# One-hot factors of a retrieval stage spread over three engines, and single dots tied to the cast stream

## The chip, the cores and the metric

The kernel runs on one core of a Trainium2 chip. The metric is the device time of one execution in microseconds (us). A core has TensorE (PE, matrix products; PEld is its loading of weights), VectorE (DVE), ScalarE (ACT), GpSimd (POOL) and SyncE (SP), each with its own queue of instructions that run in order, and DMA engines that are started from the queues of SP, ACT and POOL. Engines wait for each other by semaphores.

## The reference

A trunk of two layers over 256 tokens of width 1024. Each layer mixes tokens (gated convolution, window attention, spatial gating), then retrieves from 128 × 128 = 16384 single-neuron experts. Only the retrieval matters here:

```python
q = (t @ w_pq).reshape(T, PEER_HEADS, 2, PEER_HALF)
s = jnp.einsum('thpk,hpnk->thpn', q, sub_keys, preferred_element_type=jnp.float32)
top_s, top_i = lax.top_k(s, PEER_TOPK)
cand_s = top_s[:, :, 0, :, None] + top_s[:, :, 1, None, :]
cand_i = top_i[:, :, 0, :, None] * N_KEYS + top_i[:, :, 1, None, :]
best_s, best_pos = lax.top_k(cand_s.reshape(T, PEER_HEADS, PEER_TOPK * PEER_TOPK), PEER_TOPK)
experts = jnp.take_along_axis(cand_i.reshape(T, PEER_HEADS, PEER_TOPK * PEER_TOPK), best_pos, axis=-1)
gate = jax.nn.softmax(best_s, axis=-1)
u = expert_down[experts]
act = jax.nn.gelu(jnp.einsum('td,thkd->thk', t, u, preferred_element_type=jnp.float32), approximate=False)
wgt = (gate * act).astype(t.dtype)
vv = expert_up[experts]
return jnp.einsum('thk,thkd->td', wgt, vv)
```

For each token 8 heads choose 16 experts each: 128 pairs of a first index, a second index and a gate. The token's vector is multiplied with the chosen rows of one table, passed through a gelu, gated, and used to weight the chosen rows of another.

## The kernel before, in words

**The expert stage.** Instead of gathering rows, the kernel multiplies all tokens with all experts. The table "down" streams through in 128 chunks of 128 × 1024 (`next_chunk`, `chunk_mm`, L316 to L320). Each chunk is split into a high part (`hi`, a cast on ScalarE, L246) and a low part (`lo`, a subtraction on VectorE, L239), three buffers of each, and makes 24 matmuls: hi, lo and hi again (L318, L319, L320) for eight slices of the depth. `cast_step` makes the two parts, two chunks ahead of use, and gives them a high priority. SyncE fetches the raw chunks into seven buffers. Two chunks make a pair; after each pair ScalarE applies the gelu (`act`, `gelu`). The chunks of the conditioning weights that are due in the same stretch are held back and multiplied on VectorE right behind a low part (`Src.held`, `ada_chunk`, L204), where their place is pinned by `tc.keep_in_program_order`.

**The gates.** For 192 of the 256 tokens the chosen pairs are turned into a 128 × 128 matrix of gates per token, by a matmul of one-hots: the contraction runs over the token's 128 picks, one factor is the one-hot of the first index, the other the one-hot of the second index times the gate. The gate is kept as two 16-bit parts, high and low, so each token takes two matmuls (`gate_mm`, L1013 and L1014). Four tokens are a group; 48 groups a layer. `make_onehots` makes a group's one-hots into one of two buffers (`R_ON`): GpSimd compares the first index of each of the four tokens with a row of numbers (L1000, four instructions), VectorE compares the second index of all four in one instruction (L1003) and multiplies it with the high and with the low part (L1005, two instructions). `to_picks` (L866 to L871) transposes the picks of 128 tokens so that they lie across the partitions, in `picks` (32-bit) and `parts` (16-bit). `gate_use` multiplies the gate matrix into the activations, on VectorE (L1021) for experts that already have theirs and by a copy on ScalarE (L1024) for the rest. Groups are spread over the chunks from the one where the choosing is done (the list `fill` is empty) to chunk 124, at even chunks, some even chunks with two.

**The other 64 tokens** have their activations without gates written to memory (L1031) and are picked out per expert while the second table "up" streams through (`combine`). In layer 1 sixteen of them leave the big product (`FT` is 256 in layer 0 and 240 in layer 1); their chosen rows of "down" are gathered by GpSimd's indirect DMA (`dot_fetch`, L953, three buffers) and multiplied one by one on VectorE (`dot`, L959). `dot_plan` says at which chunk each step is issued: the fetches 5, 6 and 7 chunks after the gates' start, the first dot after 9, then one every 25/8 chunks, each followed by the fetch of the third next. `dot_where` (L948) makes the row numbers before.

**The order of the work.** In the expert stage's first half a planner fixes each engine's order: it simulates a timeline with its own costs and takes from what is ready the instruction of highest priority. So the place in the program is a priority and not a place in the queue, except for what is pinned. In the second half (`combine`) and at the seams the order is that of the program.

Of the kernel before, what the change touches and what calls it, by code (L numbers as in the profile page):

```python
# [17 lines left out]
P = 128  # L18
# [36 lines left out]
DOT_STEP = 25  # L55
# [3 lines left out]
def hybrid_trunk(ctx: ExitStack, tc: tile.TileContext, x_in, c_in, vec_in, w_ada, w_in, w_out, w_pq,  # L59
# [21 lines left out]
    iota = consts.tile([P, P], F16, name="iota")  # L81
    nc.gpsimd.iota(iota, pattern=[[1, P]], base=0, channel_multiplier=0,
                   allow_small_or_imprecise_dtypes=True)
# [13 lines left out]
    picks = consts.tile([P, S], F32, name="picks")  # L97
    parts = consts.tile([P, 3, S], F16, name="parts")
# [53 lines left out]
    R_DX = region(108 * S, D)  # L152
    R_DIX = region(127 * S + 128, 4, 16)
# [24 lines left out]
    class Src:  # L178
# [4 lines left out]
        held = []  # L183

# [34 lines left out]
    def cast_step(late=None):  # L219
# [13 lines left out]
        else:  # L233
# [20 lines left out]
            while Src.held:  # L254
                ada_chunk(*Src.held.pop(0), held=True)
        dma_ahead(k + RAW)
# [517 lines left out]
    def retrieval(layer, update, late):  # L774
# [80 lines left out]
        def to_picks(b):  # L855
# [10 lines left out]
            nc.vector.tensor_copy(picks[:, t], ps[:, 0:P])  # L866
            nc.scalar.copy(parts[:, 0, t], ps[:, P:2 * P])
            g = ps[:, 2 * P:3 * P]
            nc.scalar.activation(parts[:, 1, t], g, AF.Copy, scale=GATE_SCALE)
            nc.vector.scalar_tensor_tensor(parts[:, 2, t], g, GATE_SCALE, parts[:, 1, t],  # L870
# [53 lines left out]
    def experts(layer, rest):  # L924
# [32 lines left out]
        def dot(k):  # L957
            row = R_DOTS[k % 3]
            nc.vector.scalar_tensor_tensor(row, row, 1.0, R_DX, op0=OP.mult, op1=OP.mult,  # L959
                                           accum_out=R_DIX[:, 2, k:k + 1])  # L960
            if k + 3 < 16:
                dot_fetch(k + 3)
# [12 lines left out]
        def dot_plan(start):  # L975
            plan = {start: [lambda: nc.scalar.dma_start(dot_ids, chosen[P - alone:, 0, :])],
                    start + 2: [dot_ranks], start + 4: [dot_where]}
            for k in range(3):
                plan[start + 5 + k] = [lambda k=k: dot_fetch(k)]
            for k in range(16):  # L980
                plan.setdefault(start + 9 + k * DOT_STEP // 8, []).append(lambda k=k: dot(k))
            end = start + 9 + 15 * DOT_STEP // 8
            plan[end + 1] = [dot_acts]
            plan[end + 3] = [dot_back]
            assert end + 3 < 108
            return plan
# [5 lines left out]
        def make_onehots(g):  # L992
            tile4 = R_ON[g % 2]
            oh = tile4[:, 0].rearrange("p (i n) -> p i n", i=4)
            on = tile4[:, 1].rearrange("p (a n b) -> p a n b", a=2, b=2)
            og = [tile4[:, 2 + j].rearrange("p (a n b) -> p a n b", a=2, b=2) for j in range(2)]
            ts = slice(4 * g, 4 * g + 4)
            for i in range(4):
                t = 4 * g + i
                nc.gpsimd.tensor_scalar(oh[:, i, :], iota, picks[:, t:t + 1], None, op0=OP.is_equal)  # L1000
            wide = lambda j: parts[:, j, ts].rearrange("p (a b) -> p a b", b=2)[:, :, None, :].to_broadcast(
                [P, 2, P, 2])
            nc.vector.tensor_tensor(on, iota2[:, None, :, :].to_broadcast([P, 2, P, 2]), wide(0), op=OP.is_equal)  # L1003
            for j in range(2):
                nc.vector.tensor_tensor(og[j], on, wide(1 + j), op=OP.mult)  # L1005
            onehots[g] = oh, og

        def gate_mm(g):
            oh, og = onehots.pop(g)
            ps = bank("g", 2)  # L1010
            for i in range(4):
                dst = ps[:, i * P:(i + 1) * P]
                nc.tensor.matmul(dst, oh[:, i, :], og[0][:, i // 2, :, i % 2], start=True, stop=False)  # L1013
                nc.tensor.matmul(dst, oh[:, i, :], og[1][:, i // 2, :, i % 2], start=False, stop=True)  # L1014
# [343 lines left out]
```

## Time and profile before

| | us |
|---|---|
| median of three runs | 1742.49 (1738.18 to 1743.83) |
| the profiled execution | 1742.29 |
| its span in the profile | 1740.6 |
| PE busy | 1704.4 (98%) |
| DVE busy | 1454.9 (84%) |
| ACT busy | 905.4 (52%) |
| POOL busy | 868.1 (50%) |

The span runs from the first to the last instruction of the program. In it layer 0 chooses and multiplies with "down" from about 150 to 584 us and with "up" to about 880; layer 1 does so from about 1000 to 1432 and 1740. Gate matmuls run from 283 to about 569 and from 1129 to 1418. "A <- B" behind a group of instructions says that engine or line A sat idle until B ended. Matmuls are pipelined, so their durations overlap; where PE works without a pause the time from one to the next counts.

### The profile page before, as it was taken

To read this page: it belongs to the slowest core of one execution; us is meant where nothing else is said; L and a number is where in the kernel's file an instruction comes from. 1 tells how busy PE (TensorE), PEld (TensorE's weight loads), DVE (VectorE), ACT (ScalarE), POOL (GpSimd) and SP (SyncE) were. 2 spreads that over 40 slices of the span, in tenths; PEclk is the share of its full clock that TensorE was granted. 3 is DMA by queue.
4 is the path that set the end of the run, shared out by engine and by line. 5 is a ranking of instruction groups with operands and counts; after the bars stand their busy time and mean duration, and the time that the engine had idled before them with its cause. 6 is when DMAs were issued, how large, how long until landed. Compare 5 with 4: busy or idle time off the path is not lost.

```text
span 1740.6 us, 32411 instructions
## 1 busy us (share of the span) xinstructions
PE 1704.4 (98%) x11856; PEld 1555.4 (89%) x11856; DVE 1454.9 (84%) x2722; ACT 905.4 (52%) x1472; POOL 868.1 (50%) x713
## 2 busy tenths in 40 slices
PE   7999999999999999999999999998999999999998
PEld 6889999999999888888888999998999998888887
DVE  6858998788889699999966699968778878999996
ACT  2436455544444555555657555543554555555553
POOL 1000206588999377776100011259879847777630
PEclk9999999999999999999999999998999999999999
DMA  9965568888878799999954556687766668999993
GB/s 381 341 231 170 164 206 279 300 265 253 259 252 257 241 349 397 367 356 379 332 152 128 170 155 188 210 268 255 254 202 200 205 201 285 387 382 351 358 373 111
DMA packets 162562, 461.94 MB, mean 265 GB/s; under 512 B 51585, under 2 KB 53009, under 8 KB 161250
## 3 DMA queue, kind: packets, MB, share of 16 engines
q1 hardware_dynamic: 99936, 363.38, 61.6%
q0 software_dynamic: 26240, 88.36, 13.6%
q10 hardware_dynamic: 36226, 8.13, 2.2%
q8 instruction: 93, 1.52, 0.4%
q14 instruction: 67, 0.55, 0.1%
HBM read 449.16 MB, written 10.57 MB: 264 GB/s over the span
## 4 chain that ended last, share of the span: by engine, by line
PE 85%; DVE 9%; issue 2%; DMA 2%; POOL 1%; ACT 1%; SPq 0%; DVEq 0%; POOLq 0%; ACTq 0%
PE acc L1123 34%; PE ch L318 13%; PE ch L319 13%; PE ch L320 13%; PE ch L316 3%; DVE lo L239 3%; PE g L1013 1%; PE g L1014 1%; PE ch L399 1%; DMA raw<-in_w_ada 1%; PE acc L320 1%; PE acc L318 1%; PE acc L319 1%; DVE arena L781 1%; POOL arena L1000 1%
## 5 line engine op out<-in xcount | busy, mean ns | idle before, releaser
L246 ACT CAST hi<-raw 128x1024 fp32r<-128x1024 f32 x554 | 581.9, 1051 | 615.0 <-PE ch L320 314.4
L239 DVE TENSOR_TENSOR lo<-raw,hi 128x1024 fp32r<-128x1024 f32 x554 | 677.4, 1227 | 153.0 <-ACT hi L246 151.5
L318 PE MATMUL ch<-hh,hi 128*128 128x256 f32 (+1 forms) x2336 | 661.4, 283 | 0.1
L319 PE MATMUL ch<-hh,lo 128*128 128x256 f32 (+1 forms) x2336 | 656.2, 281 | 4.7 <-DVE lo L239 4.7
L320 PE MATMUL ch<-hh,hi 128*128 128x256 f32 (+1 forms) x2336 | 653.5, 280 | 0.0
L1000 POOL TENSOR_SCALAR arena<-iota,picks 128x128 f16<-128x128 f16 x384 | 445.9, 1178 | 184.4 <-PE g L1014 77.5
L319 PEld LDWEIGHTS ch<-hh,lo 128*128 128x128 f32 x2336 | 443.1, 190 | 6.5 <-DVE lo L239 6.1
L318 PEld LDWEIGHTS ch<-hh,hi 128*128 128x128 f32 x2336 | 442.9, 190 | 0.7 <-ACT ungated L1030 0.4
L320 PEld LDWEIGHTS ch<-hh,hi 128*128 128x128 f32 x2336 | 443.0, 190 | 0.0
L1123 PE MATMUL acc<-hi,hh 128*128 128x512 f32 x1536 | 400.6, 395 | 0.0
L1123 PEld LDWEIGHTS acc<-hi,hh 128*128 128x128 f32 x1536 | 288.6, 188 | 68.6 <-DVE hh L1064 0.2
L1123 PE MATMUL acc<-lo,hh 128*128 128x512 f32 x1024 | 281.2, 395 | 0.0
L1082 POOL DMA_INDIRECT arena<-in_up,arena x128 | 183.9, 1437 | 111.3 <-DVE arena L1119 84.6
L1123 PEld LDWEIGHTS acc<-lo,hh 128*128 128x128 f32 x1024 | 192.6, 188 | 45.8
L1089 POOL DMA_INDIRECT arena<-act_rows,arena x128 | 176.9, 1382 | 83.0 <-PE acc L1123 44.9
L1119 DVE SCALAR_TENSOR_TENSOR arena<-arena 128x1024 f32<-128x1024 f32 x126 | 161.9, 1285 | 0.0
L204 DVE SCALAR_TENSOR_TENSOR raw<-raw,arena 128x1024 f32<-128x1024 f32 x96 | 117.1, 1224 | 9.1 <-DMA raw<-in_w_ada 5.5
L1005 DVE TENSOR_TENSOR arena<-arena,parts 128x512 f16<-128x512 f16 x192 | 77.0, 440 | 23.0 <-PE g L1013 23.0
L795 POOL CAST arena<-arena 128x512 f16<-128x512 uint32 x32 | 27.1, 861 | 138.4 <-DVE arena L784 106.7
L759 POOL DMA_DIRECT2D arena<-in_keys x2 | 1.1, 562 | 170.7 <-issue 117.2
L1024 ACT ACTIVATE arena<-g 128x344 f32<-128x344 f32 (+23 forms) x96 | 31.1, 325 | 77.6 <-DVE arena L1021 76.0
L1013 PE MATMUL g<-arena 128*128 128x128 f16 x384 | 55.5, 223 | 7.8 <-POOL arena L1000 7.7
(243 smaller groups left out, 1666.5 us busy)
## 6 DMA issues: line engine op xcount, KB each, us to landing
raw<-in_down SPq DMA_DIRECT2D x256, 512.0 KB, 4.5
raw<-in_up SPq DMA_DIRECT2D x256, 512.0 KB, 6.4
raw<-in_w_ada SPq DMA_DIRECT2D x96, 512.0 KB, 4.7
raw<-in_w_pq SPq DMA_DIRECT2D x32, 512.0 KB, 3.9
raw<-in_w_in SPq DMA_DIRECT2D x26, 512.0 KB, 4.4
raw<-in_w_out SPq DMA_DIRECT2D x16, 512.0 KB, 3.9
act_rows<-ungated ACTq DMA_DIRECT2D x64, 64.0 KB, 4.7
arena<-in_w_in SPq DMA_DIRECT2D x6, 512.0 KB, 9.2
```

The costliest lines, as they stand in the source:

```text
L204: op = nc.vector.scalar_tensor_tensor(raw, raw, 1.0, cact, op0=OP.mult, op1=OP.mult, accum_out=mods[layer][:, col:col + 1])
L239: nc.vector.tensor_sub(lo, raw, hi.bitcast(F32))
L246: nc.scalar.copy(hi, raw)
L318: nc.tensor.matmul(dst, hi[:, cols], k[0], start=start, stop=False, **kw)
L319: nc.tensor.matmul(dst, lo[:, cols], k[0], start=False, stop=False, **kw)
L320: nc.tensor.matmul(dst, hi[:, cols], k[1], start=False, stop=stop, **kw)
L1000: nc.gpsimd.tensor_scalar(oh[:, i, :], iota, picks[:, t:t + 1], None, op0=OP.is_equal)
L1005: nc.vector.tensor_tensor(og[j], on, wide(1 + j), op=OP.mult)
L1082: nc.gpsimd.indirect_dma_start(out=R_ROWS[slots[k]], out_offset=None, in_=rows, in_offset=bass.IndirectOffsetOnAxis(ap=where_row[:, k:k + ...
L1089: nc.gpsimd.indirect_dma_start(out=R_ACTS[:, k % (2 * GROUP), :width - T], out_offset=None, in_=act_rows[layer][:, :], in_offset=bass.Indi ...
L1119: nc.vector.scalar_tensor_tensor(R_SUM, v, w8[:, k:k + 1], R_SUM, op0=OP.mult, op1=OP.add)
L1123: nc.tensor.matmul(acc[piece], w, u[:, lo:hi], start=piece not in opened, stop=last, skip_group_check=True)
```

## The change

- The order of the matmul's factors: the first index's one-hot now carries the gate parts (`og`), the second index's is plain (`on`).
- `picks` becomes 16-bit and holds both indices of a group side by side, so that one compare on VectorE makes both one-hots of the four tokens (1024 elements, `both`).
- The eight copies of the first index's one-hot with a gate part (four tokens, high and low) are made on three engines: GpSimd makes the high parts of tokens 0 and 1, each in one instruction that compares and multiplies (from `firsts` and `parts`, without waiting for the compare on VectorE); ScalarE makes the low parts of tokens 0 and 1 and the high parts of tokens 2 and 3 by a copy with a scale per partition; VectorE makes the low parts of tokens 2 and 3 in one multiplication. `parts` becomes 32-bit, as those operands are.
- `to_picks` writes these forms: two more small copies on ScalarE for each 128 tokens.
- The dots are issued by `cast_step`, behind the low part of the chunk being cast, and pinned there; one is handed over every 3 chunks from the 14th after the gates' start, and the first three fetches come 5, 8 and 11 chunks after it.

```diff
@@ consts
-    iota = consts.tile([P, P], F16, name="iota")
-    nc.gpsimd.iota(iota, pattern=[[1, P]], base=0, channel_multiplier=0,
-                   allow_small_or_imprecise_dtypes=True)
...
-    picks = consts.tile([P, S], F32, name="picks")
-    parts = consts.tile([P, 3, S], F16, name="parts")
+    picks = consts.tile([P, S // 4, 2, 4], F16, name="picks")
+    parts = consts.tile([P, 2, S], F32, name="parts")
...
+    firsts = region(127 * S, S // 4, 2)
@@ cast_step
             while Src.held:
                 ada_chunk(*Src.held.pop(0), held=True)
+            while Src.dots:
+                Src.dots.pop(0)()
@@ to_picks
-            nc.vector.tensor_copy(picks[:, t], ps[:, 0:P])
-            nc.scalar.copy(parts[:, 0, t], ps[:, P:2 * P])
+            at = picks[:, b * P // 4:(b + 1) * P // 4]
+            nc.vector.tensor_copy(at[:, :, 0, :], ps[:, 0:P].rearrange("p (g t) -> p g t", t=4))
+            nc.scalar.copy(firsts[:, b * P // 4:(b + 1) * P // 4, :],
+                           ps[:, 0:P].rearrange("p (g t) -> p g t", t=4)[:, :, 0:2])
+            nc.scalar.copy(at[:, :, 1, :], ps[:, P:2 * P].rearrange("p (g t) -> p g t", t=4))
             g = ps[:, 2 * P:3 * P]
-            nc.scalar.activation(parts[:, 1, t], g, AF.Copy, scale=GATE_SCALE)
-            nc.vector.scalar_tensor_tensor(parts[:, 2, t], g, GATE_SCALE, parts[:, 1, t],
+            high = tmp[:, 0, :].bitcast(F16)[:, :P]
+            nc.scalar.activation(high, g, AF.Copy, scale=GATE_SCALE)
+            nc.scalar.copy(parts[:, 0, t], high)
+            nc.vector.scalar_tensor_tensor(parts[:, 1, t], g, GATE_SCALE, high,
                                            op0=OP.mult, op1=OP.subtract)
@@ dot
-            nc.vector.scalar_tensor_tensor(row, row, 1.0, R_DX, op0=OP.mult, op1=OP.mult,
-                                           accum_out=R_DIX[:, 2, k:k + 1])
+            tc.keep_in_program_order(nc.vector.scalar_tensor_tensor(
+                row, row, 1.0, R_DX, op0=OP.mult, op1=OP.mult, accum_out=R_DIX[:, 2, k:k + 1]))
@@ dot_plan
             for k in range(3):
-                plan[start + 5 + k] = [lambda k=k: dot_fetch(k)]
+                plan[start + 5 + 3 * k] = [lambda k=k: dot_fetch(k)]
             for k in range(16):
-                plan.setdefault(start + 9 + k * DOT_STEP // 8, []).append(lambda k=k: dot(k))
-            end = start + 9 + 15 * DOT_STEP // 8
+                plan[start + 14 + 3 * k] = [lambda k=k: Src.dots.append(lambda: dot(k))]
+            end = start + 14 + 45
@@ make_onehots
             tile4 = R_ON[g % 2]
-            oh = tile4[:, 0].rearrange("p (i n) -> p i n", i=4)
+            both = tile4[:, 0:2].rearrange("p k (a n b) -> p (k a) n b", a=2, b=2)
+            vals = picks[:, g].rearrange("p k (a b) -> p (k a) b", b=2)
+            nc.vector.tensor_tensor(both, iota2[:, None, :, :].to_broadcast([P, 4, P, 2]),
+                                    vals[:, :, None, :].to_broadcast([P, 4, P, 2]), op=OP.is_equal)
+            oh = tile4[:, 0].rearrange("p (a n b) -> p a b n", a=2, b=2)
             on = tile4[:, 1].rearrange("p (a n b) -> p a n b", a=2, b=2)
-            og = [tile4[:, 2 + j].rearrange("p (a n b) -> p a n b", a=2, b=2) for j in range(2)]
-            ts = slice(4 * g, 4 * g + 4)
-            for i in range(4):
-                t = 4 * g + i
-                nc.gpsimd.tensor_scalar(oh[:, i, :], iota, picks[:, t:t + 1], None, op0=OP.is_equal)
-            wide = lambda j: parts[:, j, ts].rearrange("p (a b) -> p a b", b=2)[:, :, None, :].to_broadcast(
-                [P, 2, P, 2])
-            nc.vector.tensor_tensor(on, iota2[:, None, :, :].to_broadcast([P, 2, P, 2]), wide(0), op=OP.is_equal)
-            for j in range(2):
-                nc.vector.tensor_tensor(og[j], on, wide(1 + j), op=OP.mult)
-            onehots[g] = oh, og
+            og = [tile4[:, 2 + j].rearrange("p (a b n) -> p a b n", a=2, b=2) for j in range(2)]
+            t = 4 * g
+            for i in range(2):
+                nc.gpsimd.tensor_scalar(og[0][:, 0, i, :], iota2[:, :, 0], firsts[:, g, i:i + 1],
+                                        parts[:, 0, t + i:t + i + 1], op0=OP.is_equal, op1=OP.mult)
+                nc.scalar.activation(og[1][:, 0, i, :], oh[:, 0, i, :], AF.Copy,
+                                     scale=parts[:, 1, t + i:t + i + 1])
+                nc.scalar.activation(og[0][:, 1, i, :], oh[:, 1, i, :], AF.Copy,
+                                     scale=parts[:, 0, t + 2 + i:t + 3 + i])
+            nc.vector.tensor_tensor(og[1][:, 1], oh[:, 1],
+                                    parts[:, 1, t + 2:t + 4][:, :, None].to_broadcast([P, 2, P]), op=OP.mult)
+            onehots[g] = on, og
@@ gate_mm
-                nc.tensor.matmul(dst, oh[:, i, :], og[0][:, i // 2, :, i % 2], start=True, stop=False)
-                nc.tensor.matmul(dst, oh[:, i, :], og[1][:, i // 2, :, i % 2], start=False, stop=True)
+                for j in range(2):
+                    nc.tensor.matmul(dst, og[j][:, i // 2, i % 2, :], on[:, i // 2, :, i % 2], start=j == 0,
+                                     stop=j == 1)
```

More of the change, by code (lines that the diff above doesn't have):

```diff
@@ L54 @@
 FT = (S, 240)
-DOT_STEP = 25
 @with_exitstack
@@ L183, in hybrid_trunk @@
         held = []
+        dots = []
     def dma_ahead(upto):
@@ L993, in make_onehots @@
             tile4 = R_ON[g % 2]
-            oh = tile4[:, 0].rearrange("p (i n) -> p i n", i=4)
-            on = tile4[:, 1].rearrange("p (a n b) -> p a n b", a=2, b=2)
-            og = [tile4[:, 2 + j].rearrange("p (a n b) -> p a n b", a=2, b=2) for j in range(2)]
-            ts = slice(4 * g, 4 * g + 4)
-            for i in range(4):
-                t = 4 * g + i
-                nc.gpsimd.tensor_scalar(oh[:, i, :], iota, picks[:, t:t + 1], None, op0=OP.is_equal)
-            wide = lambda j: parts[:, j, ts].rearrange("p (a b) -> p a b", b=2)[:, :, None, :].to_broadcast(
-                [P, 2, P, 2])
-            nc.vector.tensor_tensor(on, iota2[:, None, :, :].to_broadcast([P, 2, P, 2]), wide(0), op=OP.is_equal)
-            for j in range(2):
-                nc.vector.tensor_tensor(og[j], on, wide(1 + j), op=OP.mult)
-            onehots[g] = oh, og
+            both = tile4[:, 0:2].rearrange("p k (a n b) -> p (k a) n b", a=2, b=2)
[3 more added lines that the diff above has]
+            oh = tile4[:, 0].rearrange("p (a n b) -> p a b n", a=2, b=2)
+            on = tile4[:, 1].rearrange("p (a n b) -> p a n b", a=2, b=2)
+            og = [tile4[:, 2 + j].rearrange("p (a b n) -> p a b n", a=2, b=2) for j in range(2)]
[10 more added lines that the diff above has]
+            onehots[g] = on, og
         def gate_mm(g):
-            oh, og = onehots.pop(g)
+            on, og = onehots.pop(g)
             ps = bank("g", 2)
```

## The prediction

> **What bounds the kernel now.** I read the busy shares first, then the waits, then the time in stretches of whole chunks. A chunk is the 24 matmuls of one block of 128 expert rows (eight depth slices, three products each); in the expert stage it is the unit of time.
>
> ```profile
> span 1740.6 us, 32411 instructions
> ## 1 busy us (share of the span) xinstructions
> PE 1704.4 (98%) x11856; PEld 1555.4 (89%) x11856; DVE 1454.9 (84%) x2722; ACT 905.4 (52%) x1472; POOL 868.1 (50%) x713
> ```
>
> PE is the bound; an edit on other engines can only win back what PE stands idle or runs slowly. So I looked for where it does. In the next view the columns after the stretch are its length and each engine's busy time with its count, then the granted clock and the DMA share.
>
> ```profile
> core 0: us, PE busy (x) PEld busy (x) DVE busy (x) ACT busy (x) POOL busy (x), PEclk, DMA share, GB/s
> 271.00:569.00 298.00, 298.00 (x2667) 296.19 (x2667) 256.64 (x442) 147.79 (x287) 239.58 (x196) 1.00 0.83 268
> 1093.91:1118.03 24.12, 24.12 (x218) 24.12 (x217) 24.05 (x59) 12.10 (x19) 0.00 (x0) 1.00 0.71 213
> 1121.00:1148.88 27.88, 27.76 (x251) 27.50 (x250) 19.91 (x37) 16.86 (x27) 17.26 (x13) 1.00 0.61 183
> 1148.88:1178.38 29.50, 26.62 (x236) 25.65 (x235) 22.32 (x35) 13.47 (x26) 18.04 (x12) 1.00 0.92 328
> 1178.38:1233.35 54.97, 47.19 (x413) 45.27 (x410) 43.80 (x80) 21.82 (x44) 52.65 (x46) 0.91 0.79 255
> 1239.24:1275.06 35.82, 35.82 (x348) 35.64 (x346) 26.86 (x48) 18.73 (x38) 27.70 (x29) 1.00 0.69 210
> 432.40:470.51 38.11, 38.11 (x346) 37.86 (x345) 33.93 (x60) 18.49 (x37) 33.09 (x27) 1.00 0.83 260
> ```
>
> The first row is the whole gate stage of layer 0: PE has no idle time at all, and the last row, twelve chunks of it, none either. The row 1239 to 1275 is the settled gate stage of layer 1, the same. Between them lies the loss: from 1148.88 to 1233.35, where layer 1's dots and its first gate groups run. The waits name two causes.
>
> ```profile
> engine line waited for: us in total, times, longest us
> ACT hi L246 <- PE ch L320: 314.4, 244, 6.1
> ...
> POOL arena L1000 <- PE g L1014: 77.5, 33, 17.1
> ACT arena L1024 <- DVE arena L1021: 76.0, 82, 2.9
> ...
> DVE arena L959 <- DMA arena<-in_down_rows,arena: 13.1, 8, 3.8
> ...
> POOL arena L953 <- DVE arena L959: 9.8, 6, 3.0
> PEld L1013 <- POOL arena L1000: 9.4, 8, 2.1
> ...
> PEld ch L319 <- DVE lo L239: 6.1, 7, 1.9
> ```
>
> Gate matmuls (L1013) wait for GpSimd's compares (L1000), eight times; and chunks wait for low parts (L239), while a dot (L959) stands ahead of them on VectorE waiting for its gathered rows. The chain of waits shows the same stretch from the other side:
>
> ```profile
> 1155.74 8.26 DMA arena<-in_down_rows,arena
> ...
> 1188.51 1.42 POOL arena L1000
> 1201.34 2.86 POOL arena L1000 x2
> ...
> 1205.48 1.83 POOL arena L1000
> ```
>
> **How large the loss is.** A chunk without gates takes 24.12/9 = 2.68 us (second row: nine chunks). In the settled stretch of layer 1, twelve chunks and seven gate groups take 35.82, so a group adds (35.82 − 12 × 2.68)/7 = 0.52. The stretch from 1148.88 holds nine chunks and two groups: 24.12 + 1.04 = 25.2 expected, 29.50 taken, **4.3 lost**. The one from 1178.38 holds fourteen chunks and nine groups: 37.5 + 4.7 = 42.2 expected, 54.97 taken, **12.8 lost**. Of these 12.8, 54.97 − 47.19 = 7.8 is PE standing idle; the other 5.0 is the clock, granted at 0.91 here and at 1.00 in every other row (0.09 × 54.97 = 4.9). All told 17.1 can be won, and 0.6 more from 1121.00 (ten chunks and one group, 27.3 expected, 27.88 taken), which I leave alone. By the Trainium skill ("TensorE: Matmul & The Clock Gate", Part 1) the clock drops to half after an idle window of about 3.4 us and returns after a busy one of that length; with it the 5.0 would go as soon as the idle stretches go, which is how I count it from the rows anyhow, and short leftover waits would cost only themselves.
>
> **Why GpSimd is late there, and what the change does to it.**
>
> ```profile
> L1000 POOL TENSOR_SCALAR arena<-iota,picks x384: 590/872/2768, 272.6 to 1413.6; 128x128 f16<-128x128 f16 x192
> ...
> L953 POOL DMA_INDIRECT arena<-in_down_rows,arena x16: 937/1674/1872, 1148.4 to 1212.1; - x16
> ...
> DMA to landing us min/median/max: 4.4/6.9/8.8
> ```
>
> ```profile
> L1000 POOL TENSOR_SCALAR arena<-iota,picks 128x128 f16<-128x128 f16 x384 | 445.9, 1178 | 184.4 <-PE g L1014 77.5 <-DVE picks L866 53.9 <-DVE arena L849 52.5
> ...
> L1005 DVE TENSOR_TENSOR arena<-arena,parts 128x512 f16<-128x512 f16 x192 | 77.0, 440 | 23.0 <-PE g L1013 23.0
> ...
> L1003 DVE TENSOR_TENSOR arena<-iota,parts 128x512 f16<-128x512 f16 x96 | 42.1, 449 | 0.0
> ...
> L843 DVE TENSOR_TENSOR arena<-arena 128x1024 f16<-128x1024 f16 x8 | 5.4, 678 | 0.0
> ...
> L415 DVE TENSOR_TENSOR arena<-arena 128x256 f32<-128x256 f32 x18 | 6.5, 419 | 0.0
> ...
> L563 ACT ACTIVATE arena<-arena,m 128x128 f32<-128x128 f32 x16 | 6.2, 391 | 5.2 <-DVE m L560 5.2
> ...
> L1030 ACT ACTIVATE ungated<-ch 128x128 f32<-128x128 f32 x64 | 17.6, 276 | 0.0
> ```
>
> GpSimd's compare takes 0.59 at best, 1.18 in the mean. A group needs four: 4.71 us. A group comes every 35.82/7 = 5.1 us, so GpSimd is at its limit even without dots, and each dot puts a row fetch of 1.67 on the same queue, which moreover waits for the dot three before it (9.8 in all). That is the 12.8.
>
> *GpSimd after:* two instructions a group, each a compare and a multiplication. No row shows a two-operation form. Below: the mean of one operation, 1.18; above: twice that, 2.36. The 0.59 beyond the best case is time that some other instruction held it up, and that doesn't double with the work in it, so the inside is 0.59 to 1.18 plus 0.59; I take 1.5. A group is then 3.0 instead of 4.71 (bounds 2.4 to 4.7), and with a fetch of 1.67 every three chunks (0.96 a group) still under 5.1. By the Trainium skill ("GPSIMD Engine Reference", section 3.1) up to two operations per element are limited by the port and cost what one does; no run here shows it; by it a group would be 2.4 and nothing of the 12.8 would stay.
>
> *VectorE after:* one compare of 1024 elements (0.68, L843) and one multiplication of 256 with a 32-bit factor (0.42, L415; not below 0.22, half of L1005) replace 0.45 + 2 × 0.44 = 1.33. That is 1.10, or 22 us less busy time over 96 groups, all behind a busy PE: nothing won.
>
> *ScalarE after:* four activations with a per-partition scale a group: 0.39 each (L563 has such an operand; L1030 without one is the lower end at 0.28), so 1.1 to 1.56. In the settled stretch of layer 1 that makes 18.73 + 7 × 1.56 = 29.7 of 35.82 (83%), in layer 0 18.49 + 10.9 = 29.4 of 38.11 (77%). It is hidden behind PE as long as casts come in time. The cover is the third buffer of `hi`: the slot is free when the chunk three before has ended (the 314.4 us of waiting above), and its low part is needed two chunks later.
>
> ```profile
> L239 DVE TENSOR_TENSOR lo<-raw,hi 128x1024 fp32r<-128x1024 f32 x554 | 677.4, 1227 | 153.0 <-ACT hi L246 151.5
> L246 ACT CAST hi<-raw 128x1024 fp32r<-128x1024 f32 x554 | 581.9, 1051 | 615.0 <-PE ch L320 314.4 <-PE acc L1123 147.9 <-DVE lo L239 99.5
> ...
> L959 DVE SCALAR_TENSOR_TENSOR arena<-arena x16: 1211/1224/1451, 1154.2 to 1217.7; 128x1024 f32<-128x1024 f32 x16
> L959 DVE DVE_READ_ACCUMULATOR arena<-arena x16: 76/78/84, 1155.4 to 1218.8; 128x1 f32 x16
> ```
>
> Two chunks are 5.36 at least; cast and low part take 1.05 + 1.23; 3.1 is to spare in layer 1.
>
> *New waits.* ScalarE's four now wait for VectorE's compare, which waits for PE to have left the buffer; behind them on ScalarE stand the next cast, the gelu and the gating copy (L1024, already waiting 76.0 in all). PE's gate matmuls wait for three engines instead of two. I charge 0.5 us in all for this, with 0 and about 5 (96 groups by 0.05) as ends.
>
> *Dots.* They leave the time when the planner had packed sixteen of them into 65 us (1154 to 1219) and come one per three chunks, each behind a low part that was due anyway. A dot's rows have three buffers, so some nine chunks or 25 us to arrive, against 6.9 to land: the 13.1 of waiting should go, and with it the 4.3. The single wait for the row numbers ahead of the first fetch stays; I leave 0.5 for it. The dots now fall on the settled gate stage: VectorE there becomes 26.86 − 1.6 + 4 × 1.30 (L959 with the reading of its sum) = 30.5 of 35.82, still hidden. I charge 1.0 for collisions.
>
> *The rest:* two more small copies at each of the four evacuations of the picks, on ScalarE at half load (16.86 of 27.88): nothing. The gate matmuls are as many and of the same shapes: nothing. Layer 0: nothing to win, the first row says.
>
> **The sum.** The profiled execution took 1742.3 (span 1740.6 and 1.7 around it); the median shown is 1742.5, so it stands for the runs. 1742.3 − 12.8 − 4.3 + 0.5 + 0.5 + 1.0 = 1727.2; I keep 1.3 of the 12.8 as not recovered, since the end of the dots (their write and read back on ScalarE's queue) lay inside it and only moves: **1728.5**. Its own range is 1722 to 1736.
>
> **Rivals.**
>
> *GpSimd stays last.* If the joint operation costs the upper end, 2.36, a group still takes 4.7, and with a fetch of 0.96 a group that is 5.7 against 5.1: the gate matmuls wait as before while the dots last. For it: no row shows such an instruction, and GpSimd's times range from 590 to 2768 ns. Against: the part beyond 0.59 is delay, not work. Only the 4.3 is won: 1742.3 − 4.3 = 1738.0, no change that can be told. 14%.
>
> *ScalarE's queue becomes the delay (slower).* Place: a group of layer 1 whose compare stands on VectorE behind a low part and a dot. Then ScalarE's four start after 1.23 + 1.30 + 0.68 and hold the next cast until 1.56 later: 4.8, which is 1.7 over the 3.1 to spare, and PE stands for it at L319. Sixteen dots make 27: 1728.5 + 27 = 1755.5; from twelve such groups on it is slower than before by what can be told. For: ScalarE at 83%, in order, and waits chained over three engines. Against: the planner places the four where it expects the compare done, and casts go ahead by priority. 13%.
>
> *The dots do not do what is said.* Only the dot is pinned, not its fetch; if fetches slip behind GpSimd's one-hots, VectorE waits at a fixed place, as the 13.1 did. It costs the 4.3 again: 1732.8, inside the forecast's range.
>
> **How the numbers follow.** Forecast with its range 73%, GpSimd last 14%, ScalarE late 13%. A difference under 0.3% (5.2 us, 1737.3 to 1747.7) can't be told here. Of the second case a little falls under 1737.3. So faster 0.74, same 0.13, slower 0.13. The range goes from 1721 (everything regained, with a few microseconds of scatter) to 1744, which takes in the second case and the small ends of the third.
>
> **What would show it.** Right: in layer 1 the stretch of the first ten or so gate groups has PE busy throughout at a clock of 1.00; no row of L1013's successor waits for GpSimd by more than 1 us in all; the dots lie about 8 us apart; GpSimd's instruction is near 1.5 in the mean; layer 0's gate stage still takes 298 for the same chunks. Wrong: GpSimd's mean over 2.2, or casts that wait for VectorE's compare with PE idle at the low-part matmul, or gaps at the gate matmuls ended by ScalarE.

## The result and the profile after

The changed kernel takes 1724.25 us (median; 1723.44 to 1725.37) against 1743.16 us for the kernel before on the same chip: a ratio of 0.9896, with a 95% interval from 0.9875 to 0.9918. The forecast was 1728.5 us with a range from 1721 to 1744. The profiled execution took 1724.26 us.

First the profile of after, its span and busy shares:

```profile
span 1722.6 us, 32340 instructions
...
PE 1696.9 (99%) x11856; PEld 1552.3 (90%) x11856; DVE 1440.4 (84%) x2626; ACT 1015.3 (59%) x1864; POOL 714.0 (41%) x520
```

PE issues the same 11856 matmuls. ScalarE is 110 us busier and GpSimd 154 us less busy, but neither was the bound. What counts is where PE stops losing time. Here are the stretches of after that answer to those shown of before, in the same columns (length, each engine's busy time, granted clock, DMA share): layer 0's gate stage, nine or ten chunks without gates, then three stretches of layer 1 in which gate groups run.

```profile
core 0: us, PE busy (x) PEld busy (x) DVE busy (x) ACT busy (x) POOL busy (x), PEclk, DMA share, GB/s
271.00:569.00 298.00, 298.00 (x2665) 295.89 (x2664) 253.37 (x407) 202.51 (x483) 150.79 (x100) 1.00 0.83 268
1093.00:1118.00 25.00, 25.00 (x226) 25.00 (x225) 20.75 (x49) 12.10 (x19) 0.00 (x0) 1.00 0.72 221
1148.00:1174.00 26.00, 26.00 (x244) 25.91 (x243) 14.86 (x24) 16.31 (x36) 7.31 (x7) 1.00 0.77 262
1176.92:1216.32 39.40, 39.40 (x386) 39.20 (x385) 29.54 (x49) 29.37 (x70) 18.91 (x16) 1.00 0.69 221
1222.22:1257.86 35.64, 35.64 (x345) 35.46 (x343) 30.33 (x50) 26.48 (x66) 29.71 (x19) 1.00 0.78 257
```

In layer 1 PE now works without a gap at a clock of 1.00 where it stood idle for 10.7 us of 84.5 before. In layer 0 the same 298 us hold practically the same number of matmuls (2665 and 2667).

The waits of after that concern the change:

```profile
POOL arena L1008 <- PE g L1024: 194.7, 62, 21.7
...
ACT arena L1010 <- DVE arena L1001: 32.8, 73, 1.9
...
DVE arena L1001 <- PE g L1024: 19.0, 29, 1.4
...
POOL arena L958 <- DVE arena L964: 4.5, 2, 2.3
```

GpSimd waits for PE now (L1008 is its compare with factor, L1024 the gate matmul), not PE for GpSimd: no wait of PE names L1008 at all. VectorE's dots (L964) have no wait for their rows either.

How long the two expert stages take from end to end is read from the high-part matmul's weight loads: the last two numbers before the form are the start of the first and of the last one. First before, then after:

```profile
L318 PEld LDWEIGHTS ch<-hh,hi x2336: 186/188/333, 149.6 to 1431.4; 128*128 128x128 f32 x195
```
```profile
L318 PEld LDWEIGHTS ch<-hh,hi x2336: 186/188/194, 149.7 to 1414.6; 128*128 128x128 f32 x195
```

That is 1281.8 before and 1264.9 after: 16.9 us of the 18.0 between the two profiled executions. The rest lies behind the last chunk, where 309.2 us (1740.6 − 1431.4) became 308.0. In the profiles of the ten experiments below this tail takes between 308.0 and 309.5 us, with the change and without it, so I do not put the 1.2 us down to the change. I call the time between the two starts "the expert stages" from here on.

### The profile page after: what moved, and what is told of

It is laid out like the page before. It is cut to its first block, busy times and chain, and to the rows that moved or that the text cites. A ratio compares the mean times of both kernels' runs of the same rounds, so it can differ in the third digit from the quotient of the medians.

```text
span 1722.6 us, 32340 instructions
## 1 busy us (share of the span) xinstructions
PE 1696.9 (99%) x11856; PEld 1552.3 (90%) x11856; DVE 1440.4 (84%) x2626; ACT 1015.3 (59%) x1864; POOL 714.0 (41%) x520
## 4 chain that ended last, share of the span: by engine, by line
PE 88%; DVE 9%; DMA 1%; ACT 1%; issue 1%; SPq 0%; DVEq 0%; ACTq 0%
PE acc L1134 35%; PE ch L318 14%; PE ch L319 13%; PE ch L320 13%; PE g L1024 3%; PE ch L316 3%; DVE lo L237 3%; PE ch L399 1%; DMA raw<-in_w_ada 1%; PE acc L318 1%; PE acc L320 1%; PE acc L319 1%; DVE arena L781 1%; DVE arena L782 1%; DVE arena L784 1%; PE acc L316 1%
## 5 line engine op out<-in xcount | busy, mean ns | idle before, releaser
L318 PE MATMUL ch<-hh,hi 128*128 128x256 f32 (+1 forms) x2336 | 660.7, 283 | 0.0
L318 PEld LDWEIGHTS ch<-hh,hi 128*128 128x128 f32 x2336 | 441.2, 189 | 0.3 <-issue 0.3
L1008 POOL TENSOR_SCALAR arena<-iota,arena,parts 128x128 f16<-128x128 f16 x192 | 293.1, 1534 | 307.9 <-PE g L1024 194.7
L1093 POOL DMA_INDIRECT arena<-in_up,arena x128 | 180.1, 1407 | 111.5 <-DVE arena L1130 81.7
L1100 POOL DMA_INDIRECT arena<-act_rows,arena x128 | 180.5, 1410 | 85.3 <-issue 35.6
L1010 ACT ACTIVATE arena<-arena,parts 128x128 f16<-128x128 f16 x192 | 75.6, 395 | 33.7 <-DVE arena L1001 32.8
L1001 DVE TENSOR_TENSOR arena<-iota,picks 128x1024 f16<-128x1024 f16 x96 | 68.0, 710 | 19.1 <-PE g L1024 19.0
L1012 ACT ACTIVATE arena<-arena,parts 128x128 f16<-128x128 f16 x192 | 74.2, 388 | 0.0
```

The lines of the kernel that those rows point to most:

```text
L318: nc.tensor.matmul(dst, hi[:, cols], k[0], start=start, stop=False, **kw)
L1008: nc.gpsimd.tensor_scalar(og[0][:, 0, i, :], iota2[:, :, 0], firsts[:, g, i:i + 1], parts[:, 0, t + i:t + i + 1], op0=OP.is_equal, op1=OP. ...
L1010: nc.scalar.activation(og[1][:, 0, i, :], oh[:, 0, i, :], AF.Copy, scale=parts[:, 1, t + i:t + i + 1])
L1093: nc.gpsimd.indirect_dma_start(out=R_ROWS[slots[k]], out_offset=None, in_=rows, in_offset=bass.IndirectOffsetOnAxis(ap=where_row[:, k:k + ...
L1100: nc.gpsimd.indirect_dma_start(out=R_ACTS[:, k % (2 * GROUP), :width - T], out_offset=None, in_=act_rows[layer][:, :], in_offset=bass.Indi ...
```

## The experiments

All kernels do the whole computation unless the expectation says otherwise. Times are medians; the ratio is to the kernel before on the same chip. The expert stages are read from the row shown above in each kernel's own profile.

| run | time, us | ratio to before (95%) | expert stages, us |
|---|---|---|---|
| before | 1740.7 to 1743.2 | 1 | 1281.8 |
| after | 1724.25 | 0.9896 (0.9875 to 0.9918) | 1264.9 |
| 1 dots alone | 1737.16 | 0.9977 (0.9965 to 0.9988) | 1280.1 |
| 2 one-hots alone | 1744.02 | 1.0006 (0.9993 to 1.0019) | 1285.0 |
| 3 before without dots | 1735.02 | 0.9963 (0.9949 to 0.9978) | 1265.1 |
| 4 after, dots not pinned | 1741.23 | 0.9997 (0.9980 to 1.0014) | 1279.8 |
| 5 after, dots pinned, old places | 1724.36 | 0.9899 (0.9883 to 0.9916) | 1266.3 |
| 6 GpSimd's copies twice | 1795.54 | 1.0308 (1.0282 to 1.0335) | 1336.9 |
| 7 all eight copies on ScalarE | 1728.34 | 0.9923 (0.9901 to 0.9944) | 1269.2 |
| 8 dots in both layers | 1715.47 | 0.9843 (0.9825 to 0.9862) | 1257.9 |
| 9 as 8, GpSimd none | 1712.82 | 0.9839 (0.9819 to 0.9858) | 1253.6 |
| 10 as 8, GpSimd one copy | 1710.87 | 0.9824 (0.9806 to 0.9843) | 1251.2 |

**1. The dots alone** (the kernel before, with the dots' new places and their pin):

```diff
+            while Src.dots:
+                Src.dots.pop(0)()
...
-            nc.vector.scalar_tensor_tensor(row, row, 1.0, R_DX, ...)
+            tc.keep_in_program_order(nc.vector.scalar_tensor_tensor(row, row, 1.0, R_DX, ...))
-                plan[start + 5 + k] = [lambda k=k: dot_fetch(k)]
+                plan[start + 5 + 3 * k] = [lambda k=k: dot_fetch(k)]
-                plan.setdefault(start + 9 + k * DOT_STEP // 8, []).append(lambda k=k: dot(k))
+                plan[start + 14 + 3 * k] = [lambda k=k: Src.dots.append(lambda: dot(k))]
```

> The kernel before with the dots alone moved: behind low parts, pinned, one per three chunks; the one-hots as before (four compares on GpSimd). Theory A, two causes (the prediction's): GpSimd needs 4 x 1.18 = 4.71 us a group, and with a row fetch of about 1.4 every three chunks (0.8 a group) 5.5 against the 5.1 that a group may take, so gate matmuls go on waiting for GpSimd, now spread over the 130 us that the dots take: 0.4 x 26 groups = 10 lost, 4.3 won and 3 to 6 more: about 1735 to 1739. Theory B, one cause, the crowding of the dots: GpSimd with four compares is good enough wherever dots do not crowd it (layer 0 has no idle time with it), so nearly all of the 17 is won by moving the dots: 1726 to 1728, PE busy throughout in the first gate groups of layer 1, clock 1.00 there.

Measured: 1737.16 us, as theory A has it. The first gate groups run clean, and the loss comes back later, where two gate groups fall together among the dots: all twelve waits of gate matmuls for GpSimd lie at the four such places between 1252 and 1368 us. In the windows of this kernel, the first gate groups and then two such places with their neighbours:

```profile
1176.00:1216.00 40.00, 40.00 (x384) 39.82 (x383) 31.37 (x57) 21.18 (x42) 32.06 (x32) 1.00 0.66 214
...
1246.00:1262.00 16.00, 13.96 (x118) 13.21 (x117) 10.65 (x21) 6.45 (x13) 15.64 (x17) 0.89 0.68 224
1318.00:1334.00 16.00, 13.96 (x119) 13.19 (x118) 11.00 (x20) 6.22 (x13) 15.60 (x17) 0.89 0.67 221
```

and its waits (L1003 is GpSimd's compare here, L1016 the gate matmul):

```profile
PEld L1016 <- POOL arena L1003: 9.9, 13, 1.5
...
PE g L1016 <- POOL arena L1003: 7.5, 12, 1.3
```

GpSimd is busy for 15.6 of 16 us there and PE waits for it, 7.5 us in all; behind three of the four places the trace shows the clock at half for 3.4 us, which costs another 5.1. So beside the pinned dots four compares a group are still too much. The prediction's sum for GpSimd (5.7 us a group against 5.1) had the shortage in every group; it shows only where two groups come together.

**2. The one-hots alone** (the changed kernel with the dots as before: neither pinned nor moved; the reverse of the diff above):

> The changed kernel with the dots as before (unpinned, fetches at 5, 6 and 7, a dot per 25/8 chunks from the ninth, placed by the planner), the one-hots on three engines. Theory A: the 12.8 is GpSimd's load and goes, the 4.3 of dots that wait for their rows ahead of low parts stays: 1743 - 12.8 = 1730, gaps only ahead of low-part matmuls. Theory B: the crowding stays, VectorE is as full as before while sixteen dots stand in 65 us, and the gate matmuls now wait for VectorE's compare and ScalarE instead of GpSimd: 1736 to 1742.

Measured: 1744.02 us: nothing gained, and more than either theory had. Its waits (L963 is the dot, L238 the low part, L318 its matmul):

```profile
DVE arena L963 <- DMA arena<-in_down_rows,arena: 17.9, 8, 6.6
...
PEld ch L318 <- DVE lo L238: 15.7, 7, 4.1
...
PE ch L318 <- DVE lo L238: 14.4, 7, 4.0
```

PE no longer waits for GpSimd; it waits 14.4 us for low parts instead, against 4.7 in before. One case from the timelines of VectorE and PE in this kernel (start, length, idle time before and its releaser in brackets):

```profile
1165.20 1.23 DVE L963 SCALAR_TENSOR_TENSOR arena<-arena 128x1024 f32<-128x1024 f32 x1 [6.56 <-DMA arena<-in_down_rows,arena]
...
1166.55 1.21 DVE L238 TENSOR_TENSOR lo<-raw,hi 128x1024 fp32r<-128x1024 f32 x1
```
```profile
1167.82 0.38 PE L318 MATMUL ch<-hh,lo 128*128 128x240 f32 x1 [3.18 <-DVE lo L238]
```

The dot stands on VectorE for 6.56 us until its rows have come; the low part that PE needs stands behind it, in order; PE waits 3.18 us. This kind of gap was known from before (13.1 us of such waits), but the faster one-hots did not leave it at 4.3 us: all of the loss is in it now. Every kernel is planned anew, though (the first dot starts at 1165.2 us here, at 1154.2 in before). How much of the 14.4 lay hidden behind GpSimd's waits in before, and how much the new order made, these runs do not separate.

**3. Before without the dots** (no row fetches, a small fill in place of each multiplication):

```diff
-            nc.vector.scalar_tensor_tensor(row, row, 1.0, R_DX, ..., accum_out=R_DIX[:, 2, k:k + 1])
-            if k + 3 < 16:
-                dot_fetch(k + 3)
+            nc.vector.memset(R_DIX[:, 2, k:k + 1], 0.0)
...
-                plan[start + 5 + k] = [lambda k=k: dot_fetch(k)]
+                pass
```

> The kernel before without the sixteen row fetches and their multiplications in layer 1 (sums set to zero; the sixteen tokens' part of the output is left out). Both theories: the dots are needed for the loss, so the stretch from layer 1's first gate group on runs without idle time though GpSimd still makes four compares a group: 1743 - 17 = 1726 (1724 to 1728). A third, that GpSimd's compares or the seam of the choosing alone cause waits there, expects a part of the 12.8 to stay: 1730 or more, with gate matmuls that wait for GpSimd.

Measured: 1735.02 us, but the time alone misleads: this kernel reaches its first expert chunk 9.8 us later than before (159.4 against 149.6), because the planner put the first transfers in another order (its chain of waits begins with `vec` and `w_in`, that of before with `w_ada`). The expert stages take 1265.1 us, as after. So four compares a group, with no dots, lose nothing:

```profile
L318 PEld LDWEIGHTS ch<-hh,hi x2336: 186/188/193, 159.4 to 1424.5; 128*128 128x128 f32 x195
```
```profile
1131.00:1183.00 52.00, 51.87 (x471) 51.59 (x470) 34.14 (x55) 30.29 (x52) 26.62 (x20) 1.00 0.72 241
1183.00:1226.00 43.00, 43.00 (x417) 42.77 (x417) 31.87 (x59) 22.49 (x44) 31.11 (x33) 1.00 0.66 205
```

Four compares without dots cost nothing, then; unpinned dots cost the whole even beside the lighter one-hots (run 2); pinned dots beside four compares still cost most of it (run 1). The loss needs the dots, and with them it goes only when both are seen to.

**4 and 5. Pin or place?** Run 4 keeps the new places in the plan, but the dots are neither handed to the cast nor pinned; run 5 keeps the pin, behind the low part, at the old places.

```diff
 run 4
-            tc.keep_in_program_order(nc.vector.scalar_tensor_tensor(row, row, 1.0, R_DX, ...))
+            nc.vector.scalar_tensor_tensor(row, row, 1.0, R_DX, ...)
-                plan[start + 14 + 3 * k] = [lambda k=k: Src.dots.append(lambda: dot(k))]
+                plan[start + 14 + 3 * k] = [lambda k=k: dot(k)]
 run 5
-                plan[start + 5 + 3 * k] = [lambda k=k: dot_fetch(k)]
+                plan[start + 5 + k] = [lambda k=k: dot_fetch(k)]
-                plan[start + 14 + 3 * k] = [lambda k=k: Src.dots.append(lambda: dot(k))]
+                plan.setdefault(start + 9 + k * DOT_STEP // 8, []).append(
+                    lambda k=k: Src.dots.append(lambda: dot(k)))
```

> The changed kernel with the dots at the same places in the program (from the 14th chunk after the start, every third) but neither pinned nor behind a low part: the planner places them. If the pace in the program is what matters: 1724 within 2, dots some 8 us apart. If the planner pulls them forward again as it did before, they stand closer than 8 us, wait for their rows ahead of low parts, and part of the 4.3 comes back: 1726 to 1729.

> The changed kernel with the dots pinned behind low parts but at the program's old places (fetches at 5, 6 and 7 chunks after the start, dots from the ninth, one per 25/8). Theory P, the pin is what matters, because without it the planner pulls the dots ahead to where their rows have not landed: 1724 within 2, dots about 8.5 us apart from about 1192 us on, no wait for rows. Theory Q, the later start and the spread fetches matter too (dots from the ninth chunk fall on the first gate groups): VectorE waits for rows at pinned places and a few microseconds of the 17 come back: 1728 or more.

Measured: 1741.23 us for run 4, nearly all of the gain lost where its expectation had 1729 at most, and 1724.36 for run 5, as theory P has it. The instructions of the dot's line in run 4, in run 5 and in after (count, shortest, median and longest duration in ns, first and last start):

```profile
L964 DVE SCALAR_TENSOR_TENSOR arena<-arena x16: 1210/1224/1516, 1161.7 to 1223.0; 128x1024 f32<-128x1024 f32 x16
```
```profile
L965 DVE SCALAR_TENSOR_TENSOR arena<-arena x16: 1210/1218/1223, 1191.7 to 1330.6; 128x1024 f32<-128x1024 f32 x16
```
```profile
L964 DVE SCALAR_TENSOR_TENSOR arena<-arena x16: 1211/1218/1222, 1206.4 to 1340.9; 128x1024 f32<-128x1024 f32 x16
```

Without the pin the planner moves the dots forward again whatever the plan says: sixteen in 61 us, 4.1 apart. With it they lie 9.3 apart in run 5 (old places) and 9.0 in after (new places), and both win the same. The pin behind the low part is what the gain needs; the new places are not.

The rate of the unpinned dots explains itself. They come 4.1 to 4.2 us apart in before (1154.2 to 1217.7), in run 2 (1165.2 to 1227.6) and in run 4, so each of the three row buffers turns round in about 12.5 us. Of this, from the rows of before, the dot is 1.2, the issue of its fetch on GpSimd 1.67 and the landing 6.9: 9.8, before any wait in GpSimd's queue. The dots thus run as fast as rows can come, each waiting on VectorE ahead of a low part, and a faster GpSimd can shorten at most the 2.7 that are left over. This last step is worked out, not run on its own.

That rate also gives the size of the loss. Counted in the traces, PE multiplies 16.3 chunks and 8 gate groups from the first dot to the last in before, 14.7 and 9 in run 2, 15.4 and 9 in run 4. At 2.68 us a chunk and 0.52 a group that is 47.8, 44.1 and 46.0 us; 63.4, 62.4 and 61.4 were taken. So 15.6, 18.3 and 15.4 us are lost while the dots run, with four compares on GpSimd or with two instructions.

**6 and 7. How near are GpSimd and ScalarE to being the bound?** Run 6 issues each of GpSimd's instructions twice, with the same result; run 7 puts all eight copies on ScalarE.

```diff
 run 6
+                for _ in range(2):
                     nc.gpsimd.tensor_scalar(og[0][:, 0, i, :], iota2[:, :, 0], firsts[:, g, i:i + 1], ...)
 run 7
-                nc.gpsimd.tensor_scalar(og[0][:, 0, i, :], iota2[:, :, 0], firsts[:, g, i:i + 1], ...)
+                nc.scalar.activation(og[0][:, 0, i, :], oh[:, 0, i, :], AF.Copy, scale=parts[:, 0, t + i:t + i + 1])
-            nc.vector.tensor_tensor(og[1][:, 1], oh[:, 1], parts[:, 1, t + 2:t + 4]..., op=OP.mult)
+            for i in range(2):
+                nc.scalar.activation(og[1][:, 1, i, :], oh[:, 1, i, :], AF.Copy,
+                                     scale=parts[:, 1, t + 2 + i:t + 3 + i])
```

> The changed kernel with each of GpSimd's two instructions of a group issued twice: four of 1.53 us, 6.1 a group, where a group may take 5.1 in layer 1 and 5.4 in layer 0. Theory A: GpSimd is the limit then: gate matmuls wait for it, 1.0 x 48 and 0.7 x 48 us: 1724 + 80 = about 1805; if only the delays by VectorE are shared and four take 4 x 1.2 as before, 1735 to 1750. Against it, that GpSimd's one-hots never bound anything: 1724 within 3.

> The changed kernel with all eight copies of a group on ScalarE (none on GpSimd, no multiplication on VectorE). By durations ScalarE needs 18.7 - 7 x 4 x 0.39 is already in it in the settled stretch of the changed kernel (26.5 of 35.6), so four more a group make 26.5 + 10.9 = 37.4 of 35.6: over, with PE waiting: 0.26 us a group and more where casts come late, 1735 to 1760. If what counts is the spacing from start to start (0.29 in a row of such activations), the load is 7 x 8 x 0.29 = 16 and about 16 for the rest, 32 of 35.6, and the time stays at 1724 to 1728.

Measured: 1795.54 us for run 6, 1728.34 for run 7. In run 6 the gate matmuls wait for GpSimd again (L1009 is its line there):

```profile
L1009 POOL TENSOR_SCALAR arena<-iota,arena,parts 128x128 f16<-128x128 f16 x384 | 553.3, 1452 | 135.1 <-ACT parts L874 57.2 <-DMA raw<-in_down 56.2 <-PE g L1025 20.6
...
L1025 PE MATMUL g<-arena 128*128 128x128 f16 x768 | 68.4, 224 | 49.6 <-POOL arena L1009 47.3 <-ACT arena L1036 2.2
```

Four instructions of 1.45 are 5.8 us a group against the 5.1 that a group has in layer 1 and 5.4 in layer 0: 71 us lost, which is theory A's case, 10 us under its sum (it had 1.53 for an instruction). In after two of 1.53 are 3.1. In run 7 ScalarE is 33.0 us busy of 36 in the settled stretch of layer 1 and PE still has no gap there; only some 4 us are lost over the whole kernel, which fits the case of the expectation that counts 0.29 from start to start (32 of 35.6, 1724 to 1728):

```profile
1222.00:1258.00 36.00, 36.00 (x345) 35.64 (x343) 27.68 (x43) 33.00 (x92) 3.94 (x4) 1.00 0.85 273
```

**8 to 10. A faster version.** A pinned dot costs PE nothing in layer 1, so sixteen tokens can leave the big product of layer 0 too (run 8). Runs 9 and 10 then take two or one of GpSimd's two copies to ScalarE.

```diff
 run 8
-FT = (S, 240)
+FT = (240, 240)
 run 10, beside that (run 9: ScalarE for both)
-                nc.gpsimd.tensor_scalar(og[0][:, 0, i, :], iota2[:, :, 0], firsts[:, g, i:i + 1], ...)
+                if i:
+                    nc.gpsimd.tensor_scalar(og[0][:, 0, i, :], iota2[:, :, 0], firsts[:, g, i:i + 1], ...)
+                else:
+                    nc.scalar.activation(og[0][:, 0, i, :], oh[:, 0, i, :], AF.Copy, scale=...)
```

> The changed kernel with sixteen tokens' dots in layer 0 too, so that layer 0's 128 chunks multiply 240 columns instead of 256. PE wins 128 x (2.85 - 2.68) = 22 us if all is hidden. VectorE in layer 0's gate stage is busy 253 of 298 and gets 16 x 1.30 = 21 more in 282: 97%. If VectorE carries that: 1703 to 1708. If VectorE (with the held conditioning chunks, 48 of them in layer 0) becomes the bound, low parts come late and a part is given back: 1710 to 1724.

> e8_dots_both (dots in both layers) with GpSimd's two copies of each gate group on ScalarE, so ScalarE makes six and VectorE two, and GpSimd none; all of the computation is there. In e8's layer 0 the gate matmuls wait for GpSimd's copies 6.8 us at the matmuls and 8.1 us at their weight loads, and its chunks are about 10 us longer than 2.68 us each plus their gate matmuls. Theory A: GpSimd is what limits e8's layer 0 (its copies are stretched by VectorE's sixteen more multiplications, mean 1.755 us against 1.534). Then this comes to 1715.5 - (8 to 10) + (2 to 4, what eight copies on ScalarE lost in e7) = 1707 to 1711, and no PE wait names L1008. Theory B: VectorE itself limits there (it is 97 to 100% busy from 380 to 480 us): then the waits come back ahead of low parts or behind the compare, and the time is 1714 to 1720.

> e8_dots_both with one of GpSimd's two copies of each gate group on ScalarE, so GpSimd makes one, ScalarE five and VectorE two; all of the computation is there. Theory A (GpSimd limits e8's layer 0): half its work is enough to take it off the end, and ScalarE's five cost no wait: 1715.5 - (8 to 10) = 1705 to 1709, below e9. Theory B (VectorE limits): 1713 to 1718.

Measured: 1715.47, 1712.82 and 1710.87 us. Run 8's time lies in the second of the ranges expected (1710 to 1724), but not for the reason given: its waits of PE name GpSimd, not VectorE.

```profile
PEld L1024 <- POOL arena L1008: 8.1, 7, 1.8
...
PE g L1024 <- POOL arena L1008: 6.8, 7, 1.7
```

Layer 0 from 276 to 580 us in run 8, then in run 10:

```profile
276.00:580.00 304.00, 296.83 (x2747) 292.21 (x2746) 277.61 (x444) 203.63 (x489) 216.19 (x116) 0.99 0.87 294
```
```profile
276.00:580.00 304.00, 301.92 (x2788) 297.15 (x2788) 280.97 (x450) 220.01 (x543) 129.22 (x70) 1.00 0.89 302
```

PE stands idle for 7.2 us in the first and 2.1 in the second, and no wait of PE names GpSimd in runs 9 and 10: GpSimd was what limited run 8. Both medians lie between the two theories' ranges, though, so theory A had the mechanism and too large a saving: 2.7 and 4.6 us by the medians, 4.3 and 6.7 by the expert stages, where its ranges had 4.5 to 8.5 and 6.5 to 10.5. Run 10 beats both kernels: 1.8% faster than the kernel before on its chip, where after is 1.0% faster on its own, and its expert stages are 13.7 us shorter than those of after. Between runs 8, 9 and 10 the intervals overlap; there only the profiles tell.

## Why the prediction was right, and where it was not

**The time** came 4.2 us under the forecast. Of the 17.1 us that could be won nearly all came (the expert stages are 16.9 shorter), and the four allowances I set against it (0.5 for the wait before the first fetch, 0.5 for new waits, 1.0 for collisions of dots, 1.3 not recovered: 3.3 in all) were not needed: PE has no gap in any of the stretches shown. The total did not hang on how the 17.1 is split: it is what the stretches had lost, and the change takes both causes away. The 0.6 from 1121.00, "which I leave alone", went too: the first gate matmuls come later there now.

**"All told 17.1 can be won", as 12.8 + 4.3: the step that failed.** I took the 12.8 for GpSimd's compares and the 4.3 for the dots' rows, and added them as two separate losses. The waits of before had been read rightly: in the stretch from 1148.88 PE waits for low parts alone (2.9 us), in that from 1178.38 for GpSimd alone (7.7 us):

```profile
PE ch L319 <- DVE lo L239: 2.9, 4, 1.7
```
```profile
PE g L1013 <- POOL arena L1000: 7.7, 7, 2.0
```

But the terms hold in one order only. Dots first and one-hots then: 1741.6 (before, on the chip of run 1) − 1737.2 = 4.4, and 1737.2 − 1724.3 = 12.9, taken on another chip. One-hots first: nothing (1744.0), and the dots then 19.8. Without dots there is no loss even with four compares (run 3). That 4.4 and 12.9 come so close to both terms is in part luck: in the profiled executions the expert stages have 1.7 and 15.2, and what run 1 still loses lies at other places than the 12.8 did. What stood in place of the sum: two limits, the dots' rows (a dot every 4.1 us, each ahead of a low part) and GpSimd's load, either of which alone keeps most of the loss or all of it. So the first step wins little or nothing, and the second nearly everything. My own rival "GpSimd stays last", whose price was that only the 4.3 is won (1738.0), comes out as run 1 measured it (1737.2), there with four compares.

**GpSimd, 1.5 us an instruction: right.** In after, from its groups and its line:

```profile
L1008 POOL TENSOR_SCALAR arena<-iota,arena,parts 128x128 f16<-128x128 f16 x192 | 293.1, 1534 | 307.9 <-PE g L1024 194.7 <-ACT parts L874 57.2 <-DMA raw<-in_down 55.4
...
L1010 ACT ACTIVATE arena<-arena,parts 128x128 f16<-128x128 f16 x192 | 75.6, 395 | 33.7 <-DVE arena L1001 32.8 <-DVE arena L835 0.6
...
L1001 DVE TENSOR_TENSOR arena<-iota,picks 128x1024 f16<-128x1024 f16 x96 | 68.0, 710 | 19.1 <-PE g L1024 19.0
...
L1014 DVE TENSOR_TENSOR arena<-arena,parts 128x256 f16<-128x256 f16 x96 | 39.5, 424 | 0.1
```
```profile
L1008 POOL TENSOR_SCALAR arena<-iota,arena,parts x192: 787/1626/3333, 275.9 to 1394.9; 128x128 f16<-128x128 f16 x192
```

1.534 in the mean. The best case is 0.787 against 0.590 for the compare alone, so the instruction with two operations has 0.2 more of work (it also takes a second factor and reads every second number of its row; no run separates these). The rest of the mean (0.75, against 0.59 before) is delay, close to my split (0.59 to 1.18 of work, 0.59 of delay). The Trainium skill ("GPSIMD Engine Reference", section 3.1) has up to two operations an element cost what one does; in the trace the whole instruction costs more, in the best case and in the mean (1.534 against 1.178).

**VectorE and ScalarE: right, ScalarE's share too high.** VectorE's 0.68 and 0.42 measured 0.71 and 0.42, and its stretch with dots 30.3 of 35.6 (30.5 forecast). ScalarE's 0.39 is its duration, 0.395; but in a row the next starts sooner, as its timeline shows:

```profile
1193.59 0.39 ACT L1012 ACTIVATE arena<-arena,parts 128x128 f16<-128x128 f16 x1
1193.88 0.39 ACT L1010 ACTIVATE arena<-arena,parts 128x128 f16<-128x128 f16 x1
1194.17 0.39 ACT L1012 ACTIVATE arena<-arena,parts 128x128 f16<-128x128 f16 x1
```

0.29 from start to start. So a group costs 1.2 us instead of 1.56, and ScalarE is busy for 26.5 us of the stretch instead of 29.7. The rival that ScalarE is late did not come, and run 7 shows why it is far off: even eight copies in place of four cost about 4 us, not 27.

**The dots: right in effect, the pin being the part that works.** They lie 9.0 us apart ("about 8": I had left out the gate matmuls between the chunks), without a wait for rows. That only the dot is pinned and not its fetch did no harm. **The clock: half right.** With the gaps gone it is 1.00 in these stretches. "Short leftover waits would cost only themselves" is not so; see the last section.

## What to carry to other kernels

Two waits that lie in the same stretch are not two terms of a sum: ask for each what PE would wait for if the other alone were gone, and price the pair. Where a planner is free to pull work forward, an instruction that waits for a transfer can be put ahead of the transfer's end (runs 2 and 4), and then holds up everything behind it on its queue. Pin it behind work that is due anyway, with its fetch long before; the same trick may then pay a second time (run 10). An engine far from its limit on the average (GpSimd, 50%) can still end the stretch that counts.

## What the runs showed of the hardware

**Short gaps close together can halve the clock as a long one does.** In run 1, from PE's timeline (L1016 and L1017 are gate matmuls, L321 to L323 those of a chunk):

```profile
1253.41 0.23 PE L1016 MATMUL g<-arena 128*128 128x128 f16 x1 [0.78 <-POOL arena L1003]
...
1254.38 0.23 PE L1016 MATMUL g<-arena 128*128 128x128 f16 x1 [0.68 <-POOL arena L1003]
...
1254.95 0.23 PE L1016 MATMUL g<-arena 128*128 128x128 f16 x1 [0.29 <-POOL arena L1003]
...
1255.53 0.29 PE L1016 MATMUL g<-arena 128*128 128x128 f16 x1 [0.29 <-POOL arena L1003]
...
1256.46 0.41 PE L321 MATMUL ch<-hh,hi 128*128 128x240 f32 x1
1256.67 0.41 PE L322 MATMUL ch<-hh,lo 128*128 128x240 f32 x1
...
1258.79 0.28 PE L323 MATMUL ch<-hh,hi 128*128 128x240 f32 x1
1258.91 0.27 PE L321 MATMUL ch<-hh,hi 128*128 128x240 f32 x1
```

Four waits of 0.29 to 0.78, 2.0 us in all with a pair of short matmuls after each, and from 1255.5 to 1258.8 the matmuls of the chunk start 0.21 apart instead of 0.11. The waits cost another 1.6 us (half of 3.3). The granted clock of 0.89 in this window is that. In run 2 the single wait of 3.18 us shown above has the same behind it: from 1168.5 to 1171.9 the matmuls start 0.21 apart. But in run 1 two waits close together, 0.83 and 0.74 us before 1293.8 and 1294.8, have no slow stretch behind them:

```profile
1286.00:1302.00 16.00, 14.43 (x142) 13.99 (x142) 12.91 (x25) 7.37 (x14) 15.80 (x16) 1.00 0.66 220
```

So these runs do not show how much idle time it takes. The Trainium skill ("TensorE: Matmul & The Clock Gate", Part 1) speaks of an idle window of about 3.4 us; before the slow stretch at 1255.5 no single wait was longer than 0.8, so the length of the slow stretch agrees and the condition as I had read it does not.

**GpSimd is slow where VectorE works on two large inputs.** Worked out from the single instructions in the trace of before, by what VectorE is doing when a compare starts: the 129 that start while a low part, a dot or a held conditioning chunk is running take 1.83 us in the mean, the other 255 take 0.85, and of these the 101 that start with VectorE idle take 0.61. A long compare meets more of VectorE's work, but its length can't change what runs at its start. And none of the 129 ends sooner than 0.46 us after the VectorE instruction that it met, so little of its 0.59 us of work is done beside it. In after it is 2.06 (100) against 0.97 (92), and none of the 100 ends sooner than 0.68 us after. No run took VectorE's work away alone; with sixteen more dots in layer 0 (run 8) GpSimd's mean went from 1.534 to 1.755. The Trainium skill ("SBUF — State Buffer", the section on two separate sides) states that a VectorE instruction with two inputs and a GpSimd instruction that reads shut each other out for their whole length; the trace agrees for GpSimd as the one that waits.
